# A hybrid attention block: one step's difference in a hand-written filler schedule, and a wider share for PE in the last normalisation

## The chip, the core and the metric

The kernel runs on one core of a Trainium2 chip. A core has five engines with their own instruction streams: PE (TensorE, matrix products into the accumulator banks, PSUM), DVE (VectorE), ACT (ScalarE), POOL (GpSimd) and SP (SyncE, which here only issues DMAs). Each engine takes its instructions in program order and waits on semaphores for the others. The metric is the time of one execution in device microseconds; lower is better.

## The reference

One layer of an encoder block on 1024 tokens of width 1024, float32 in and out. One projection gives the queries, keys, values and gates of two groups of heads:

```python
h = jnp.einsum('bsd,de->bse', x, w_in[layer])
q_a, k_a, v_a, z_a, q_b, k_b, v_b, z_b = jnp.split(h, SPLIT_POINTS, axis=-1)
y_a = neighborhood_attention(q_a, k_a, v_a, rel_bias)      # per head; 8 heads, window 8 x 16 on a 16 x 64 grid, learned bias
y_b = windowed_gqa_with_sink(rotary(q_b), rotary(k_b), v_b, sink)  # 8 query heads, 2 key heads, |i - j| <= 128
mixed = jnp.concatenate([y_a * silu(z_a), y_b * silu(z_b)], axis=-1)
y = jnp.einsum('bse,ed->bsd', mixed, w_out[layer])
x = layer_norm(DEEPNORM_ALPHA * x + y, ln_gain, ln_bias)
```

All heads are 64 wide. The last line, the normalisation over the 1024 columns of a row, is what the second part of the change concerns; the projections of `k_a` and `q_a` are what the first part concerns.

## The kernel before, in words

To keep float32 accuracy with 16-bit products, every operand is held as a high and a low float16 part, and a product is three matmuls: high x high, high x low, low x high.

**Projection.** The 2688 columns besides the values are cut into 21 pieces of 128 columns, named in `ORDER` (L30): `zb0`, `z0`, ... `k3`, `q3`, `z3`. The digit is a pair of heads; `k`, `q`, `z` belong to group "a" (neighbourhood attention), names with `b` to group "b". `project` (L358) makes one piece in two halves of 512 tokens, each 8 k-tiles x 3 products = 24 matmuls of 512 columns into one bank (L379), then `evac` hands the bank to ACT and DVE: for `q` and `k`, ACT writes the high part (L257) and DVE the low part (L263), for each of the two heads; for `k`, POOL then copies each part to the other half of the partitions (L295). For a gate `z`, ACT and DVE compute the SiLU (L341, L342). The weights of a piece are split in two halves by `w_split`: ACT makes the high part (L199), POOL the low one (L204, L205). The last eight pieces' weights were loaded earlier, for their sums, and stay on the chip.

**Attention.** The first six pieces are projected before it. The other 15 (`FILL`) are fillers: `project` is a generator that gives up control after every matmul, and the main loop pumps it a few matmuls at a time between the pieces of attention, to keep PE busy. The loop has 128 steps, one for each unit: a unit is 128 queries of one head, 64 units of group "b" first, then 64 of "a", 16 for each pair of heads. At step i it emits, in this order:

- the scores of unit i on PE, two matmuls (L816, L817), and on DVE bias, minimum and scale into `sn` (L826);
- when it is due, on PE the transposes of an earlier output (L901) and the value products of four units that are 9 to 6 steps old (L881, 36 matmuls);
- for unit i-1, ACT's high part (L852), DVE's low part (L853) of the probabilities, and a DMA transpose of both (L856), issued on SP;
- fillers, then ACT's exponential of unit i (L842), queued work of the splits, and fillers again.

Unit 112 is the first that uses `k3` and `q3` (its step calls `need` for their splits), unit 113 the first that uses the second half of `q3`. `z3` is needed when the first output of the pair is gated. Units of "a" need their bias tables (loaded on SP at L784 seven steps ahead, scaled on POOL at L788) and gathered values `va` (loaded on SP at L740). The order of all this is written out by hand: from here up to the end of attention each engine executes in the order in which the program emits. SP issues transposes, `va`, bias and output-weight loads in one queue.

How many fillers a step gets is set by `FILL_AT` (L36): entry n is the step at which filler n starts, and it is spread evenly until the next entry. Entries 12, 13, 14 and 15 are `k3`, `q3`, `z3` and the first output tiles. `pump_to(u)` pumps the total due by step u.

**Output.** Eight row tiles of 128 tokens. The first banks of the output projection (L1031) are fillers at the end of attention (`out_head`); `final` does the rest. After the residual (L1077, with column sums at L1080), rows are normalised. For tiles 0 to 6 `norm` shares the work among DVE, ACT and POOL. For the last tile nothing is left to hide behind, so `norm_last` splits its 1024 columns in three, at `WP` (L51):

- HP, the first `WP` columns: POOL has multiplied them by the gain (`norm_ahead`, L1099) as soon as their half of the row was there. PE then computes scale, shift and bias as three float32 products into one bank: identity x bias ahead of time (L1104), and with two diagonal matrices `dr` and `dn` (reciprocal deviation, and minus mean times it; made on ACT at L1109, L1110) `dr` x row (L1111) and `dn` x gain (L1112). ACT copies the bank (L1114) and stores it from its own queue (L1118).
- H0, the next 256 columns, and H1, the rest: DVE computes both in two operations each (L1106 and L1113, then L1116), and SP stores them (L1117).

The last tile's second half of output columns comes in three pieces of 256, 128 and 128 columns.

Of the kernel before, what the change touches and what calls it, by code (L numbers as in the profile page):

```python
# [32 lines left out]
NS = 21 - NPRO  # L33
NR = 8
FILL = ORDER[NPRO:]
FILL_AT = [0, 8, 17, 25, 33, 41, 49, 57, 66, 74, 81, 89, 97, 105, 112, 121, 123.5, 126, 128, 131, 136]  # L36
ZTAG = {"z3": "zv", "zb3": "zc", "z2": "zs", "zb1": "zd", "zb2": "ze"}
KO = (2, 3, 4, 5, 6, 7, 0, 1)
X1_AT = ((0,), (1,), (2,), (3, 4), (5,), (6, 7), (), ())
# [8 lines left out]
M_AT = [105, 112, 118, 120]  # L48
WO_AT = [67, 71, 75, 79, 84, 88, 93, 98]
WO_LD = [16, 22, 19, 25, 36, 39, 42, 45, 48, 112, 116, 28, 130, 130, 130, 130]  # L50
WP = 256  # L51
WIN0 = (0, 8, 24, 40)
WINW = (24, 32, 32, 24)
NROW = (11, 12)
# [7 lines left out]
def hybrid_block(ctx, tc, xT, x, wt, wv, wo, bias, sink, gain, lbias, cos, sin, bmask, out):  # L62
# [856 lines left out]
    def pump_to(u):  # L919
        n = 0  # L920
        for k, c in enumerate(FILL_N):
            u0, u1 = FILL_AT[k], FILL_AT[k + 1]
            n += int(c * min(max((u - u0) / (u1 - u0), 0), 1))
# [124 lines left out]
    def final():  # L1048
# [33 lines left out]
        def row_stats(t):  # L1082
            mv = fp.tile([128, 2], F32, tag="mv", name="mv")
            nc.vector.bn_aggr(mv, stats[t][:, :8 if t == 7 else 2, :])  # L1084
            sd = fp.tile([128, 1], F32, tag="sd", name="sd")
            nc.scalar.activation(sd, mv[:, 1:2], AF.Sqrt, bias=eps)  # L1086
            return mv, sd
# [7 lines left out]

        HP, H0, H1 = slice(0, WP), slice(WP, WP + 256), slice(WP + 256, 1024)

# [3 lines left out]
        def norm_last(t):  # L1101
            ts = slice(128 * t, 128 * t + 128)
            xr = xrs[t]
            nc.tensor.matmul(pn[:, :WP], identf, bb[:, HP], start=True, stop=False)  # L1104
            mv, sd = row_stats(t)
# [4 lines left out]
            nc.scalar.activation(dn, identf, AF.Copy, scale=nmr)  # L1110
            nc.tensor.matmul(pn[:, :WP], dr, xr[:, HP], start=False, stop=False)  # L1111
            nc.tensor.matmul(pn[:, :WP], dn, gb[:, HP], start=False, stop=True)  # L1112
            nc.vector.scalar_tensor_tensor(xr[:, H1], xr[:, H1], mv[:, 0:1], gb[:, H1], op0=ALU.subtract, op1=ALU.mult)  # L1113
            nc.scalar.copy(xr[:, HP], pn[:, :WP])  # L1114
            for h in (H0, H1):
# [209 lines left out]
```

## Time and profile before

| | us |
|---|---|
| median of 3 runs | 446.71 |
| lowest and highest | 446.0, 447.76 |
| the profiled execution's own time | 446.49 |
| its span, first to last instruction | 444.7 |

The page of the profile gives busy times, the chain of work that ended last, and the costliest groups of instructions; a group's line is `line engine op out<-in xcount`. The timeline lists instructions with start and duration in microseconds, merged where they follow each other, and in brackets the engine's idle time before and who ended it. The view of waits gives for each pair, waiting engine and line `<-` releaser, the total, the number of times and the longest. Matmuls are pipelined: a 512-column matmul shows some 0.38 us from start to end, while the next one starts much earlier. A row of SP is the issue of a DMA, not the transfer; the time from issue to landing is given apart. In a table by windows the columns are the window, its length, the busy time (and count) of PE, PE's weight loads, DVE, ACT and POOL, the granted clock of PE, the DMA share and GB/s.

### The profile page before, as it was taken

What the parts mean: (1) busy time and instruction counts of PE and PEld (TensorE: products, weight loads), DVE (VectorE), ACT (ScalarE), POOL (GpSimd) and SP (SyncE); (2) the same over time, 40 slices, a digit from 0 to 9 for tenths busy, and PEclk for the clock granted to TensorE, in tenths of its full rate; (3) what the DMA queues carried; (4) which work ended last, traced back from release to release, by engine and by line L of the source; (5) the groups of instructions that cost most, each with busy time, mean ns of one, the idle gap of its engine ahead of it and who ended that gap; (6) DMA issues with size and microseconds to landing.
All of it is one profiled execution on the core that took longest, in us unless ns stands there. A gap on an engine that the chain in (4) does not pass through costs nothing.

```text
span 444.7 us, 9505 instructions
## 1 busy us (share of the span) xinstructions
PE 437.5 (98%) x3289; PEld 255.5 (57%) x3289; DVE 344.2 (77%) x849; ACT 308.3 (69%) x700; POOL 221.6 (50%) x235
## 2 busy tenths in 40 slices
PE   9999999999999999999999999999999999999994
PEld 8997754444445565655565655656555654444453
DVE  5978967438986898887988888888878837589944
ACT  5759789766499988887868887888778946302401
POOL 0110074646839558866506767765574405205740
PEclk9999999999999999999999999999999999999997
DMA  8921469984659999587978899998999998103612
GB/s 272 390 91 60 145 235 339 336 292 169 213 127 214 206 190 181 98 162 143 164 127 175 169 182 180 213 170 213 192 204 253 167 172 347 55 0 102 232 69 72
DMA packets 133841, 81.39 MB, mean 183 GB/s; under 512 B 101280, under 2 KB 113440, under 8 KB 133536
## 3 DMA queue, kind: packets, MB, share of 16 engines
q1 hardware_dynamic: 133648, 80.64, 75.4%
q8 instruction: 26, 0.43, 0.4%
q14 instruction: 23, 0.19, 0.2%
q10 hardware_dynamic: 144, 0.13, 0.1%
HBM read 50.34 MB, written 9.96 MB: 136 GB/s over the span
## 4 chain that ended last, share of the span: by engine, by line
PE 91%; DMA 3%; POOL 3%; DVE 1%; issue 1%; ACT 1%; SPq 0%; POOLq 0%; DVEq 0%; ACTq 0%
PE ps_pj L379 44%; PE ps_s L1031 9%; PE ps_s L486 6%; PE ps_t L881 6%; PE ps_pj L1031 5%; PE ps_t L1031 5%; PE ps_s L816 4%; PE ps_s L817 4%; PE ps_pj L486 3%; PE ps_t L486 3%; DMA bias<-in_bias 3%; PE ps_t L901 1%; POOL wl L205 1%; PE ps_t L412 1%; POOL ks L295 1%
## 5 line engine op out<-in xcount | busy, mean ns | idle before, releaser
L379 PE MATMUL ps_pj<-xf,wh 128*128 128x512 f16 x672 | 202.1, 379 | 0.1
L379 PE MATMUL ps_pj<-xf,wl 128*128 128x512 f16 x336 | 127.3, 379 | 0.0
L379 PEld LDWEIGHTS <-wh 128*128 128x128 f16 x672 | 63.7, 98 | 60.4 <-DVE ks L263 0.5
L842 ACT ACTIVATE ps_s<-sn,nm 128x385 f32<-128x385 f32 (+3 forms) x128 | 70.1, 548 | 25.1 <-DVE nm L826 24.6
L853 DVE SCALAR_TENSOR_TENSOR split<-ps_s,split 128x384 f16<-128x384 f32 (+2 forms) x128 | 65.7, 513 | 27.5 <-ACT split L852 25.9
L1031 PEld LDWEIGHTS <-m 128*128 128x128 f16 x432 | 40.0, 98 | 41.1 <-DVE m L939 0.2
L852 ACT ACTIVATE split<-ps_s 128x384 f16<-128x384 f32 (+2 forms) x128 | 57.8, 452 | 2.5 <-DMA tr<-split 0.2
L204 POOL TENSOR_SCALAR wr<-wr,wsc 128x512 f32<-128x512 f32 x26 | 20.6, 791 | 68.1 <-ACT wh L199 61.6
L379 PEld LDWEIGHTS <-wl 128*128 128x128 f16 x336 | 32.9, 98 | 37.4
L826 DVE CUSTOM_DVE_ANT_0 sn<-ps_s,bm,nsk 128x384 f32<-128x384 f32 (+1 forms) x64 | 40.7, 636 | 2.0 <-PE ps_s L817 1.7
L1031 PE MATMUL ps_s<-wo,m 128*128 128x512 f16 (+1 forms) x192 | 40.8, 366 | 0.0
L816 PE MATMUL ps_s<-ks,qs 128*128 128x384 f16 (+4 forms) x128 | 39.2, 306 | 0.3 <-DVE qs L263 0.3
L817 PE MATMUL ps_s<-ks,qs 128*128 128x384 f16 (+4 forms) x128 | 39.2, 306 | 0.0
L826 DVE CUSTOM_DVE_ANT_0 sn<-ps_s,bias,sg 128x264 f32<-128x264 f32 (+1 forms) x64 | 35.0, 547 | 4.5 <-issue 1.5
L881 PEld LDWEIGHTS <-tr 128*128 128x128 f16 (+1 forms) x1104 | 36.6, 98 | 2.2
L205 POOL TENSOR_TENSOR wl<-wr,wh 128x512 f16<-128x512 f32 x26 | 32.7, 1257 | 2.2
L788 POOL TENSOR_SCALAR bias<-bias,rsg 128x552 f32<-128x552 f32 (+1 forms) x24 | 19.1, 797 | 23.8 <-DMA bias<-in_bias 22.6
L295 POOL COPY ks<-ks 64x512 f16<-64x512 f16 x40 | 26.0, 661 | 7.1 <-DVE ks L263 2.8
L1086 ACT ACTIVATE sd<-mv,eps 128x1 f32<-128x1 f32 x8 | 2.4, 295 | 36.5 <-DVE mv L1084 35.2
L1031 PE MATMUL ps_pj<-wo,m 128*128 128x512 f16 (+1 forms) x144 | 26.2, 326 | 0.0
L1130 POOL TENSOR_TENSOR xr<-xr,gb 128x512 f32<-128x512 f32 x7 | 9.8, 1396 | 32.4 <-ACT xr L1127 32.4
L842 ACT ACTIVATION_READ_ACCUMULATOR ps_s<-sn,nm 128x1 f32 x128 | 24.4, 190 | 0.0
(188 smaller groups left out, 813.8 us busy)
## 6 DMA issues: line engine op xcount, KB each, us to landing
ws<-in_wt SPq DMA_DIRECT2D x15, 512.0 KB, 5.9
wr<-in_wt SPq DMA_DIRECT2D x26, 256.0 KB, 3.6
wor<-in_wo SPq DMA_DIRECT2D x22, 256.0 KB, 3.5
bias<-in_bias SPq DMA_DIRECT2D x16, 276.0 KB, 3.3
xr<-in_x SPq DMA_DIRECT2D x8, 512.0 KB, 9.6
out<-xr SPq DMA_DIRECT2D x15, 256.0 KB, 2.1
bias<-in_bias SPq DMA_DIRECT2D x8, 368.0 KB, 3.8
wvraw<-in_wv SPq DMA_DIRECT2D x9, 320.0 KB, 5.8
```

Of the source, the lines that this page charges most:

```text
L205: nc.gpsimd.tensor_sub(l, raw, h)
L295: nc.gpsimd.tensor_copy(t[o, sl], t[a, sl])
L379: nc.tensor.matmul(ps, a[:, k % 4, :], mv, start=(k == 0 and i == 0), stop=(k == KT - 1 and i == 2))
L486: nc.tensor.matmul(ps[:, :320], lh[:, ts], rh[:, cs], start=(k == ko[0] and i == 0), stop=(k == ko[-1] and i == 2))
L816: nc.tensor.matmul(ps[:, :m], q, sl[0], start=True, stop=False)
L817: nc.tensor.matmul(ps[:, :m], q, sl[1], start=False, stop=True)
L826: nc.vector.tensor_tensor_reduce(sn[:, :m], ps[:, :m], bias_t, sg[:, c:c + 1], init, op0=ALU.add, op1=ALU.min, accum_out=nm)
L842: nc.scalar.activation(pt[:, :m], sn[:, :m], AF.Exp, bias=nm, scale=-1.0, accum_out=sm[:, k:k + 1])
L852: nc.scalar.activation(hl[:, :m, 0, :c], src, AF.Copy, scale=PSCALE)
L853: nc.vector.scalar_tensor_tensor(hl[:, :m, 1, :c], src, PSCALE, hl[:, :m, 0, :c], op0=ALU.mult, op1=ALU.subtract)
L881: nc.tensor.matmul(ps[:, HD * m:HD * m + HD], a, b_, start=(i == 0), stop=(i == len(mms) - 1))
L1031: nc.tensor.matmul(ps, lh[:, ts], rh[:, cs], start=(e == EO[0] and i == 0), stop=(e == EO[-1] and i == 2))
```

## The change

Two entries of `FILL_AT` are one lower: `k3` is spread over the steps 97 to 104 instead of 97 to 105, `q3` over 104 to 111 instead of 105 to 112, and `z3` over 111 to 121 instead of 112 to 121. Nothing before step 97 or after step 121 is emitted at another place. `WP` goes from 256 to 384: HP has 384 columns, H0 stays at 256 (columns 384 to 639), and H1 shrinks from 512 to 384. The number of instructions is the same.

```diff
-FILL_AT = [0, 8, 17, 25, 33, 41, 49, 57, 66, 74, 81, 89, 97, 105, 112, 121, 123.5, 126, 128, 131, 136]
+FILL_AT = [0, 8, 17, 25, 33, 41, 49, 57, 66, 74, 81, 89, 97, 104, 111, 121, 123.5, 126, 128, 131, 136]
...
-WP = 256
+WP = 384
```

## The prediction

> **What bounds the kernel now.** I read the page first: busy time by engine and the chain of waits, for what carries the span.
>
> ```profile
> span 444.7 us, 9505 instructions
> PE 437.5 (98%) x3289; PEld 255.5 (57%) x3289; DVE 344.2 (77%) x849; ACT 308.3 (69%) x700; POOL 221.6 (50%) x235
> PE 91%; DMA 3%; POOL 3%; DVE 1%; issue 1%; ACT 1%; SPq 0%; POOLq 0%; DVEq 0%; ACTq 0%
> ```
>
> PE is the bound, so the change, which adds next to no PE work before the last rows, can only move the time through moments in which PE stands still. The view of waits, PE alone, lists them:
>
> ```profile
> PE ps_t L1111 <- ACT dr L1109: 1.8, 1, 1.8
> PE ps_s L816 <- DVE qs L263: 0.3, 1, 0.3
> ```
>
> There are two of interest, and each part of the change sits on one. The timeline around the second, PE's own, shows the scores of units 110, 112 and 113 (their first matmul, L816), and two fillers of the projection before unit 113:
>
> ```profile
> 327.05 0.28 PE L816 MATMUL ps_s<-ks,qs 128*128 128x264 f16 x1
> ...
> 330.54 0.28 PE L816 MATMUL ps_s<-ks,qs 128*128 128x264 f16 x1
> ...
> 331.41 0.59 PE L379 MATMUL ps_pj<-xf,wh 128*128 128x512 f16 x2
> 332.26 0.30 PE L816 MATMUL ps_s<-ks,qs 128*128 128x288 f16 x1 [0.26 <-DVE qs L263]
> ```
>
> One filler's price is in the chain of waits, six in a row:
>
> ```profile
> 287.39 1.29 PE ps_pj L379 x6
> ```
>
> That is 0.216 us each. Unit 113 could have started at 331.41 + 2 x 0.216 = 331.84; it started at 332.26. PE lost 0.42 us there. The timelines of ACT and DVE say why:
>
> ```profile
> 330.91 0.58 ACT L257 ACTIVATE qs<-ps_pj 64x512 f16<-64x512 f32 x1
> ```
>
> ```profile
> 327.57 0.49 DVE L826 CUSTOM_DVE_ANT_0 sn<-ps_s,bias,sg 128x264 f32<-128x264 f32 x1 [0.82 <-POOL wl L205]
> ...
> 327.99 0.55 DVE L853 SCALAR_TENSOR_TENSOR split<-ps_s,split 128x384 f16<-128x384 f32 x1
> ...
> 331.52 0.68 DVE L263 SCALAR_TENSOR_TENSOR qs<-ps_pj,qs 64x512 f16<-64x512 f32 x1 [0.81 <-ACT qs L257]
> ```
>
> The second half of q3 is complete only when unit 112 starts; its high part comes out on ACT until 331.49, its low part on DVE until 332.20, and unit 113 is the first reader of that half.
>
> **Part 1: k3 in 7 steps, q3 a step sooner, z3 over 10 steps.** No instruction is added. What moves on PE: after step 105, k3 and q3 stand (110-104) x 48/7 = 41 matmuls into q3 by step 110, where it was (110-105) x 48/7 = 34. So the scores of units 106 to 111 come behind 7 more fillers: 7 x 0.216 = 1.5 us later. By step 121 z3 is complete in both, and the shift is 0.
>
> What it saves: q3 ends before unit 111's scores. From there to unit 113 lie two pairs of scores and 9 of z3's fillers, about 2.4 us; in the trace the last low part was 332.20 - 330.54 = 1.7 us behind q3's end. The low part then has some 0.7 us to spare, and the wait goes: -0.42 us.
>
> Evacuations and weights: k3's and q3's splits on ACT and DVE (eight each), z3's weight splits (two on ACT, four on POOL) and the eight copies of k3 on POOL move ahead with the fillers; none issues a DMA here, since the last sixteen weight halves are on the chip already, and SP's order is unchanged. On POOL the bias of unit 112 drops behind z3's second weight half. POOL's list in the trace, all of these included, was through with the bias of unit 114 at
>
> ```profile
> 328.52 0.88 POOL L788 TENSOR_SCALAR bias<-bias,rsg 128x736 f32<-128x736 f32 x1
> ```
>
> that is by 329.40; the first reader, unit 112, now comes later than 330.54. I cost this at nothing; if the cover went, PE would wait the overrun at unit 112.
>
> What it costs: SP's queue. Transposes of the probabilities, the `va` loads and bias loads are issued there in order. Its timeline, the transpose of unit 109 first, then the rows behind it, and the last ten:
>
> ```profile
> 328.60 1.33 SPq L856 DMA_TRANSPOSE tr<-split  x1
> ```
>
> ```profile
> 329.99 0.57 SPq L740 DMA_DIRECT2D va<-vwin  x1
> 330.65 0.52 SPq L784 DMA_DIRECT2D bias<-in_bias  x1
> ...
> 347.56 14.93 SPq L856 DMA_TRANSPOSE tr<-split  x10
> ```
>
> From 328.60 to 362.49 the rows follow each other within 0.1 us, save 0.3 us once: the queue is full to the last transpose, and a delay ahead of it stays. And at 328.60 it has no backlog: unit 109's low part ended at 327.99 + 0.55 = 328.54, and that DVE instruction stands behind unit 110's `sn` (327.57), which stands behind unit 110's scores (327.05). Those scores now come 1.5 us later, so this transpose does too. Before it the queue was behind its data, so 0.1 of the 1.5 may be made up; I take a delay d = 1.4 us for all transposes from unit 109 on. Bounds: 0 (the data were early in some way the row hides) and 1.5; 1.4 is nearest the rows.
>
> Who waits: the value product of four units (L881, 36 matmuls over 1.05 us, nine a unit), on PE. Its two tight places, from PE's timeline, and the transposes of their fourth units (115 and 123) with the time to landing, each alone in a window:
>
> ```profile
> 346.96 1.22 PE L881 MATMUL ps_t<-va,tr 96*128 96x64 f16 x36
> ...
> 358.56 1.22 PE L881 MATMUL ps_t<-va,tr 96*128 96x64 f16 x36
> ```
>
> ```profile
> L856 SPq DMA_TRANSPOSE tr<-split x1: 1211/1211/1211, 341.5 to 341.5; - x1
> ...
> DMA to landing us min/median/max: 4.8/4.8/4.8
> ```
>
> ```profile
> L856 SPq DMA_TRANSPOSE tr<-split x1: 2615/2615/2615, 354.5 to 354.5; - x1
> ...
> DMA to landing us min/median/max: 4.2/4.2/4.2
> ```
>
> The fourth unit's matmuls start 27/36 x 1.05 = 0.79 us in: at 347.75 against a landing at 341.5 + 4.8 = 346.3, slack 1.45; and at 359.35 against 354.5 + 4.2 = 358.7, slack 0.6. With d = 1.4 the second lands at 360.1, 0.8 us behind the old start, and PE waits there whether or not it had gained 0.42 earlier. So part 1 nets max(-0.42, d - 0.6) = +0.8 us: the stall of unit 113 goes, and is late again, larger, under the transposes. Behind it PE has out-projection matmuls whose inputs come later by d too; in the trace PE waits for none of them, and I cost that at nothing.
>
> **Part 2: 384 columns instead of 256 on PE in the last rows.** The end of the timeline:
>
> ```profile
> 433.07 0.73 POOL L1099 TENSOR_TENSOR xr<-xr,gb 128x256 f32<-128x256 f32 x1 [0.21 <-DVE stats L1080]
> ```
>
> ```profile
> 436.76 0.65 PE L1104 MATMUL ps_t<-bb,identf 128*128 128x256 f32 x2
> ...
> 438.09 0.48 DVE L1106 SCALAR_TENSOR_TENSOR xr<-xr,mv,gb 128x256 f32<-128x256 f32 x1
> ...
> 438.76 0.74 DVE L1113 SCALAR_TENSOR_TENSOR xr<-xr,mv,gb 128x512 f32<-128x512 f32 x1
> ...
> 439.23 0.67 PE L1111 MATMUL ps_t<-xr,dr 128*128 128x256 f32 x2 [1.81 <-ACT dr L1109]
> ...
> 439.73 0.96 PE L1112 MATMUL ps_t<-gb,dn 128*128 128x256 f32 x2
> ...
> 440.78 0.37 ACT L1114 COPY xr<-ps_t 128x256 f32<-128x256 f32 x1 [1.41 <-PE ps_t L1112]
> 441.18 0.37 ACTq L1118 DMA_DIRECT2D out<-xr  x1
> ```
>
> ```profile
> 440.59 1.52 SPq L1117 DMA_DIRECT2D out<-xr  x1
> ```
>
> Time to landing, of that last SP store and of ACT's store:
>
> ```profile
> DMA to landing us min/median/max: 3.2/3.2/3.2
> ```
>
> ```profile
> DMA to landing us min/median/max: 2.0/2.0/2.0
> ```
>
> DVE's branch ends at 440.59 + 3.2 = 443.8, PE's at 441.18 + 2.0 = 443.2: slack 0.6. DVE's two ops of 512 columns become 384: half way between 0.48 and 0.74, each saves 0.13, so its store goes 0.26 sooner (443.5). POOL's product grows to about 1.1 us, done five microseconds ahead; L1104 grows by a third of a microsecond before `dr` exists. But L1111 and L1112 stand behind `dr`: from 439.23 to 440.69 they take 1.46 us for 256 columns. With 384 they add half of that at most, 0.73, and 0.5 if the fixed ends are left out; I take 0.55. The copy adds 0 to 0.18, taken 0.1. ACT's store is issued 0.65 later and lands at 443.9 with 2.0, the wider store perhaps 0.1 more. The last landing moves from 443.8 to about 443.95: +0.15 us. Bounds -0.26 (PE's branch stays short) and +0.6 (0.73 + 0.18, and a landing 0.3 slower).
>
> Two rows of the clock by windows bear on it:
>
> ```profile
> 439.00:440.00 1.00, 0.77 (x3) 0.72 (x4) 1.00 (x3) 0.37 (x2) 0.00 (x0) 0.92 0.00 0
> 440.00:441.00 1.00, 0.69 (x2) 0.00 (x0) 0.56 (x1) 0.22 (x1) 0.00 (x0) 0.50 0.26 79
> ```
>
> The granted clock halves at 439.84, some 2.4 us after L1104 ended (437.41), so L1112 already runs at half clock, and the added columns mostly too; 1.46 us contains that. [...]
>
> **Sum.** The profiled execution took 446.49 us, span 444.7. 446.49 + 0.8 + 0.15 = 447.4. It lies 0.2 under the median 446.71, so on that scale 447.6; I say 447.5.
>
> **Rivals.** (1) The transposes are not late enough to matter, d under 0.2: the stall is simply gone, -0.42, and the tail -0.26 to +0.15: 446.0 to 446.5. For it: softmax of earlier units was behind DVE and ACT, not PE, so their order may absorb some of 1.5 us. Against it: the zero backlog at 328.60. d = 0.6 decides between gain and loss.
> (2) The change doesn't do what it says: unit 113 waits as before, since DVE takes the low part behind unit 111's `sn` and split, which now come later. Only 0.7 us are to spare. Up to 0.4 more at unit 113, but d - 0.6 still rules: 447.5 to 448.
> (3) Slower beyond 0.5%: PE's clock drops in the middle. The place is the value product at 358.56; the tail shows a drop after 2.4 us without matmuls. It decides when transposes come 3.0 us late there, which needs a second row like the 2.6 us transpose at 354.5. The price: 2.4 us of standing still, and then each filler at 0.43 in place of 0.216; for ten fillers 2.2 us: 451. [...]
>
> **How the numbers follow.** Forecast 0.55, rival 1 0.3, rival 2 0.1, rival 3 0.05. Differences under 0.5% (2.2 us) are about what a measurement of this kernel can tell from no change, and the runs shown spread from 446.0 to 447.76. All but rival 3 lie within it: same 0.92, slower 0.06, faster 0.02. The range runs from rival 1's end, 446.0, to rival 2 with the tail's upper bound, 448.5, with 0.2 us on either side, the distance of the profiled execution from the median.
>
> **What would show it.** Right: no wait of L816 for L263 at unit 113; transposes of units 109 to 127 issued 1.4 us later against PE's fillers; a new wait of PE before the fourth quarter of the next to last L881 group; L1114 0.55 us later behind `dr`, and ACT's store landing last. Wrong: unit 109's transpose issued by 329.0, or SP's queue with gaps behind it, which would give the time back; or L1117's store still landing last.

## The result and the profile after

The changed kernel took 447.42 us (median of 20 runs, 446.25 to 448.46); the kernel before, run beside it, 446.23 us (20 runs, 445.2 to 447.76). The ratio is 1.0022 with a 95% interval of 1.0012 to 1.0031: about 1.0 us slower (1.2 between the medians), which is less than the 0.5% taken as the bound of "no change". The forecast was 447.5. The profiled execution took 447.68 us with a span of 445.9, against 446.49 and 444.7.

The page of the changed kernel, span and busy times:

```profile
span 445.9 us, 9504 instructions
PE 437.7 (98%) x3289; PEld 254.9 (57%) x3289; DVE 344.0 (77%) x849; ACT 308.1 (69%) x700; POOL 222.0 (50%) x235
```

PE is still the bound, with 0.2 us more work. The view of waits, PE alone (total, times, longest):

```profile
PE ps_t L1111 <- ACT dr L1109: 1.6, 1, 1.6
...
PE ps_t L881 <- DMA tr<-split: 0.6, 1, 0.6
```

The wait of unit 113 for the low part of `q3` (L816 <- L263) is gone, and the value product (L881) waits for a transpose. PE's timeline shows unit 113, and then two of the value products:

```profile
332.45 0.29 PE L816 MATMUL ps_s<-ks,qs 128*128 128x288 f16 x1
...
346.29 0.95 PE L881 MATMUL ps_t<-va,tr 96*128 96x64 f16 x27
347.84 0.44 PE L881 MATMUL ps_t<-va,tr 128*128 128x64 f16 x9 [0.60 <-DMA tr<-split]
...
358.68 1.45 PE L881 MATMUL ps_t<-va,tr 96*128 96x64 f16 x36
```

The first product breaks in two: 27 matmuls, then nine of the fourth unit, 115. At 1.05/36 = 0.029 us each the nine could have started at 346.29 + 0.79 = 347.08; they start at 347.84, so PE lost 0.76 us (the bracket's 0.60 counts from the modelled end of the matmul before, 0.95 us behind 346.29). The other group, with unit 123 as its fourth, takes 1.45 where an undisturbed one takes 1.22: another 0.23. Below, "standing still" is always worked out in this way.

SP's timeline shows why, the transpose of unit 109 first, then those of units 114 and 115 with an output-weight load between them:

```profile
329.86 1.22 SPq L856 DMA_TRANSPOSE tr<-split  x1
...
340.85 1.21 SPq L856 DMA_TRANSPOSE tr<-split  x1
342.12 1.54 SPq L951 DMA_DIRECT2D wor<-in_wo  x1
343.76 1.21 SPq L856 DMA_TRANSPOSE tr<-split  x1
```

Up to unit 97 the two kernels are the same. The first matmul of its scores, in the kernel before and in the changed one, shows the execution after 0.25 us ahead there:

```profile
300.58 0.29 PE L816 MATMUL ps_s<-ks,qs 128*128 128x288 f16 x1
```

```profile
300.33 0.29 PE L816 MATMUL ps_s<-ks,qs 128*128 128x288 f16 x1
```

With that taken out, unit 109's transpose is 329.86 + 0.25 - 328.60 = 1.51 us later than before, and unit 115's 343.76 + 0.25 - 341.49 = 2.5 later. The same stretch of SP in the kernel before:

```profile
341.49 1.21 SPq L856 DMA_TRANSPOSE tr<-split  x1
342.79 1.41 SPq L740 DMA_DIRECT2D va<-vwin  x1
```

Here the slow issue (1.41 in place of about 0.55) stands behind unit 115's transpose. In the changed kernel the slow one (1.54) stands ahead of it.

The end of the timeline of the changed kernel:

```profile
439.04 0.40 ACT L1109 ACTIVATE dr<-identf,rstd 128x128 f32<-128x128 f32 x1 [0.24 <-DVE rstd L1091]
...
439.59 0.89 PE L1111 MATMUL ps_t<-xr,dr 128*128 128x384 f32 x2 [1.59 <-ACT dr L1109]
...
440.31 0.81 PE L1112 MATMUL ps_t<-gb,dn 128*128 128x384 f32 x2
441.21 0.48 ACT L1114 COPY xr<-ps_t 128x384 f32<-128x384 f32 x1 [1.47 <-PE ps_t L1112]
441.72 0.37 ACTq L1118 DMA_DIRECT2D out<-xr  x1
```

The DMA view of the last microseconds, 439.4 to 445 (KB, us from issue to landing; the row of q8 is an instruction fetch, with packets, MB and share of the DMA engines):

```profile
q8 instruction: 1, 0.02, 1.1%
...
out<-xr SPq DMA_DIRECT2D x1, 192.0 KB, 1.9
out<-xr ACTq DMA_DIRECT2D x1, 192.0 KB, 3.2
out<-xr SPq DMA_DIRECT2D x1, 128.0 KB, 1.8
```

ACT's store lands last, at 441.72 + 3.2 = 444.9, and it is the slow one of the three. The same view of the kernel before (439 to 444) has the slow ones elsewhere:

```profile
q8 instruction: 1, 0.02, 1.8%
...
out<-xr SPq DMA_DIRECT2D x1, 256.0 KB, 3.2
out<-xr SPq DMA_DIRECT2D x1, 128.0 KB, 2.9
out<-xr ACTq DMA_DIRECT2D x1, 128.0 KB, 2.0
```

From the end of `dr` to the end of the span it is 445.9 - 439.44 = 6.5 us after and 444.7 - 439.08 = 5.6 before. The span's difference of 1.2 us is thus: -0.25 ahead of unit 97, -0.42 at unit 113, +0.76 + 0.23 at the transposes, +0.82 in the tail, which makes 1.14.

### The profile page after: what moved, and what is told of

Read it like the earlier page. It is cut to its first block, busy times and chain, and to the rows that moved or that the text cites. A ratio compares the mean times of both kernels' runs of the same rounds, so it can differ in the third digit from the quotient of the medians.

```text
span 445.9 us, 9504 instructions
## 1 busy us (share of the span) xinstructions
PE 437.7 (98%) x3289; PEld 254.9 (57%) x3289; DVE 344.0 (77%) x849; ACT 308.1 (69%) x700; POOL 222.0 (50%) x235
## 4 chain that ended last, share of the span: by engine, by line
PE 96%; DMA 2%; DVE 1%; ACT 0%; issue 0%; DVEq 0%; SPq 0%; ACTq 0%
PE ps_pj L379 48%; PE ps_s L1031 8%; PE ps_t L881 7%; PE ps_s L486 6%; PE ps_pj L1031 5%; PE ps_t L1031 5%; PE ps_s L816 4%; PE ps_s L817 4%; PE ps_pj L486 3%; PE ps_t L486 3%; DMA tr<-split 2%; PE ps_t L901 1%; PE ps_t L412 1%; PE ps_t L1111 0%; DVE ks L263 0%
## 5 line engine op out<-in xcount | busy, mean ns | idle before, releaser
L816 PE MATMUL ps_s<-ks,qs 128*128 128x384 f16 (+4 forms) x128 | 39.2, 307 | 0.0
L881 PEld LDWEIGHTS <-tr 128*128 128x128 f16 (+1 forms) x1104 | 36.8, 98 | 3.1 <-DMA tr<-split 0.9
```

The costliest lines, as they stand in the source:

```text
L816: nc.tensor.matmul(ps[:, :m], q, sl[0], start=True, stop=False)
L881: nc.tensor.matmul(ps[:, HD * m:HD * m + HD], a, b_, start=(i == 0), stop=(i == len(mms) - 1))
```

## The experiments

The theory: each part costs something for a reason of its own. The earlier `q3` delays the transposes in SP's full queue; the wider `WP` lengthens the branch that ends last. Rivals: one part alone makes the whole difference; the transposes' delay is beside the point and the fillers cost it in another way. The fillers alone, the columns alone, the fillers with two loads moved and the doubled dose ran on one chip beside the kernel before (446.35 us there), the other four on a second chip (446.7 us there).

**One part alone: the fillers.**

```diff
-FILL_AT = [..., 97, 105, 112, 121, ...]
+FILL_AT = [..., 97, 104, 111, 121, ...]
 WP = 256
```

> The schedule's part alone (FILL_AT of the changed kernel, WP = 256). My theory: the scores of units 106 to 111 come 1.5 us later, the transposes of units 109 to 127 follow, and PE waits for them at the fourth quarters of two value products (0.76 + 0.23 us in the changed kernel's trace) while the wait of 0.42 us at unit 113 goes: net +0.6 us against the kernel before (ratio 1.0013), with the same two waits in its trace. Rival: the loss of the changed kernel is all in the last rows; then this one is 0.4 us faster than before.

Measured: 447.47 us, ratio 1.0026 (1.0011 to 1.0041). PE's timeline at unit 115, and SP's:

```profile
346.73 0.69 PE L881 MATMUL ps_t<-va,tr 96*128 96x64 f16 x18
347.64 0.44 PE L881 MATMUL ps_t<-va,tr 128*128 128x64 f16 x9 [0.22 <-DMA tr<-split]
348.98 0.44 PE L881 MATMUL ps_t<-va,tr 128*128 128x64 f16 x9 [0.90 <-DMA tr<-split]
```

```profile
341.05 3.43 SPq L856 DMA_TRANSPOSE tr<-split  x1
344.54 0.57 SPq L951 DMA_DIRECT2D wor<-in_wo  x1
345.21 1.21 SPq L856 DMA_TRANSPOSE tr<-split  x1
```

The third and the fourth unit's quarters both wait: PE stands still 0.39 + 1.07, and 0.26 in the next group, 1.72 in all. Less the 0.42 saved that is +1.3 us in the trace, and +1.1 between the medians (0.5 to 1.8 by the ratio's interval), more than the +0.6 expected. The places differ too: PE waits for the transposes of units 114, 115 and 119, and not for unit 123's. The slow issue was unit 114's transpose here, with 3.43 us. The rival that the whole loss lies in the last rows falls.

**One part alone: the columns.**

```diff
-WP = 256
+WP = 384
```

> The last rows' part alone (WP = 384, FILL_AT of before). By the prediction +0.15 us. By the changed kernel's trace, where ACT's store took 3.2 us to land instead of 2.0, +0.8 us (1.0018) if that belongs to the 384 columns or to ACT's queue; if it was that execution's chance, between 0 and +0.3. The wait of 0.42 us at unit 113 stays in either case.

Measured: 446.79 us, ratio 1.0011 (1.0001 to 1.0020). The stall at unit 113 is there (0.42). PE also stands still for 1.47 - 1.22 = 0.25 us at one value product, ahead of the places that this document is about:

```profile
316.92 1.47 PE L881 MATMUL ps_t<-va,tr 96*128 96x64 f16 x36
```

It waits there for unit 99's transpose, which took 2.75 us to issue (at 311.97) and landed at 317.91; the matmuls that read it start at 317.96. So a slow issue can cost PE a little on the old schedule as well; this 0.25 is not the columns' price. By the medians the fillers carry the larger part of the difference and the columns about 0.4 us. By the times alone the fillers could be all of it, since this run's interval only just leaves out 1; that the columns cost something of their own rests on the tails below. The DMA view of the columns alone, 439.9 to 444.1, where no instruction fetch lies among the stores:

```profile
out<-xr SPq DMA_DIRECT2D x1, 192.0 KB, 1.9
out<-xr ACTq DMA_DIRECT2D x1, 192.0 KB, 1.9
out<-xr SPq DMA_DIRECT2D x1, 128.0 KB, 1.8
```

**The suspected cause taken away.** SP's queue holds two output-weight loads among these transposes, which nothing reads before the output. They are issued behind the last transpose instead, with the fillers of the first experiment and 256 columns; this is the third kernel below. Nothing changes on PE, ACT or DVE in what is emitted.

```diff
-WO_LD = [16, 22, 19, 25, 36, 39, 42, 45, 48, 112, 116, 28, ...]
+WO_LD = [16, 22, 19, 25, 36, 39, 42, 45, 48, 130, 130, 28, ...]
```

> The schedule's part with two output-weight loads taken out from between the transposes on SP's queue (WO_LD[9] and [10] at step 130 instead of 112 and 116; they are then issued behind the last transpose). If the loss is the transposes' delay on SP's queue, two issue slots of 0.6 us or more are given back, 0.6 us ahead of unit 111's transpose and as much ahead of unit 115's: the wait at unit 115's transpose goes, that at unit 123's shrinks below 0.3, and with the 0.42 us of unit 113 the kernel is between 0.4 us faster and equal to the one before (0.6 to 1.0 us below the schedule's part alone). Rival, the loss is not SP's queue (ACT, DVE or the transfer itself are late): no more than 0.2 us between the two.

Measured: 445.84 us, ratio 0.9997 (0.9982 to 1.0013); 1.6 us less than the fillers alone on the same chip by the medians and 1.3 by the ratios, where 0.6 to 1.0 was expected, since the fillers alone had lost more than expected. Its waits of PE have no L881 and no L816:

```profile
PE ps_t L1111 <- ACT dr L1109: 1.8, 1, 1.8
...
PE ps_pj L379 <- DVE ks L263: 0.3, 1, 0.3
```

SP's timeline, the transpose of unit 115:

```profile
342.10 2.33 SPq L856 DMA_TRANSPOSE tr<-split  x1
```

This execution is 0.51 us behind before unit 97, so unit 115's transpose comes 342.10 - 0.51 - 341.49 = 0.1 later than in the kernel before, although unit 109's is late here as in the others (330.62). Two issues taken out ahead of it have given the delay back, and the loss went with it: the way from the fillers to the lost time is SP's queue. The rival that the fillers cost it in another way falls.

**The control: the two loads alone**, with the fillers of the kernel before.

> The two output-weight loads taken out from between the transposes, on the schedule of before (FILL_AT and WP of before). Theory: before the change PE waits for no transpose, so a shorter queue on SP alone is worth nothing: within 0.2 us of before, the wait of 0.42 us at unit 113 still there and no wait of L881. Rival, the loads themselves cost PE time (or their late arrival does): 0.4 us or more in either direction.

Measured: 446.25 us, ratio 0.9996 (0.9985 to 1.0007). PE's timeline at unit 113 still shows

```profile
331.64 0.59 PE L379 MATMUL ps_pj<-xf,wh 128*128 128x512 f16 x2
332.49 0.30 PE L816 MATMUL ps_s<-ks,qs 128*128 128x288 f16 x1 [0.25 <-DVE qs L263]
```

that is 332.49 - (331.64 + 2 x 0.216) = 0.42, and no wait of L881 is there. The ratio puts it 0.2 us below the kernel before, with both signs in its interval; the medians lie 0.45 apart, more than the 0.2 expected. PE's timeline decides: its scores run 0.24 us behind the kernel before at unit 97 and the same 0.24 at unit 127, so the moved loads alone gave PE nothing. Without the earlier fillers there is nothing at the transposes to be won.

**The dose doubled.** `k3` and `q3` two steps sooner, loads where they were.

```diff
-FILL_AT = [..., 97, 105, 112, 121, ...]
+FILL_AT = [..., 97, 103, 110, 121, ...]
```

> A second dose: k3 over steps 97 to 103, q3 over 103 to 110, z3 over 110 to 121, WP = 256. Unit 110's scores come 14 fillers, 3.0 us, later than before instead of 1.5. Theory: transposes from unit 109 on are 2.9 to 3.3 us late; behind the slack of 0.6 at unit 123 that makes +2.3 to +2.7 us against before (1.005 to 1.006). Rival, the delay is made up on SP's queue or by shorter waits elsewhere: within 0.3 us of the first dose.

Measured: 448.40 us, ratio 1.0048 (1.0033 to 1.0063), +2.05 us, a little under the 2.3 to 2.7 expected. Rows of its SP and PE timelines:

```profile
331.72 1.21 SPq L856 DMA_TRANSPOSE tr<-split  x1
```

```profile
348.79 0.44 PE L881 MATMUL ps_t<-va,tr 128*128 128x64 f16 x9 [0.93 <-DMA tr<-split]
...
354.99 0.43 PE L881 MATMUL ps_t<-va,tr 96*128 96x64 f16 x9 [0.42 <-DMA tr<-split]
```

Unit 109's transpose is 3.0 us late (331.72 - 0.09 - 328.60), twice 1.5. PE stands still 2.37 us over five places, so net +1.95 in the trace. Time grows with the dose, and three fourth quarters carry most of it (1.82 of the 2.37; two third quarters carry the rest). The second step added 0.9 us between the medians, not the whole 1.5, so the rival that it stays within 0.3 us of the first dose falls.

**The third kernel again**, the same code on the second chip, since its interval held both signs.

> The earlier schedule with the two loads moved, once more, to narrow its interval. Theory: neither the wait at unit 113 nor one for a transpose: 0.4 us faster than before (ratio 0.999), and 0.4 us faster than the moved loads on the old schedule.

Measured: 445.84 us, ratio 0.9978 (0.9963 to 0.9993); no standing still at unit 113 or at a transpose. That is 0.4 us less than the moved loads on the old schedule, as expected, and 0.9 less than the kernel before by the medians, where 0.4 was expected. Its tail and DMA view (438 to 442) serve as the undisturbed tail with 256 columns:

```profile
438.24 0.67 PE L1111 MATMUL ps_t<-xr,dr 128*128 128x256 f32 x2 [1.81 <-ACT dr L1109]
...
438.75 0.59 PE L1112 MATMUL ps_t<-gb,dn 128*128 128x256 f32 x2
...
439.83 0.37 ACTq L1118 DMA_DIRECT2D out<-xr  x1
```

```profile
out<-xr SPq DMA_DIRECT2D x1, 256.0 KB, 2.1
out<-xr SPq DMA_DIRECT2D x1, 128.0 KB, 1.7
out<-xr ACTq DMA_DIRECT2D x1, 128.0 KB, 2.1
```

**The size of the columns, to the other side and further.** `WP = 192` on top of the third kernel, and `WP = 512` on the kernel before.

> The same with WP = 192. In three executions with 256 columns ACT's store was issued 1.74 us after the end of dr and landed last; SP's second store landed 0.2 us ahead. If PE's branch is the longer one already at 256 columns, 64 columns less take 0.25 us from it and put 0.13 on DVE's: 0.1 us from the end of dr to the end of the span, SP's store last. If DVE's branch is the longer one, as the prediction read it, 0.13 us more. In time, no difference that rounds can show.

> A second dose of the last rows' part: WP = 512 on the schedule of before; H1 has 256 columns. From the end of dr to the end of the span it was 4.8 to 4.9 us with 256 columns (three executions, 5.6 in a fourth) and 5.1 with 384 (6.4 in a second). If PE's branch is the bound, each 128 columns put 0.43 us on L1111 and L1112 and 0.11 on the copy: 5.6 us, and 0.8 to 1.0 us over before (1.002). If the tail is set by what a store takes to land, whatever the columns: no more than 0.3 over before.

Measured: 446.03 us, ratio 0.9989 (0.9976 to 1.0002), with 192, and 447.32 us, 1.0013 (1.0000 to 1.0025), with 512. PE's last row and ACT's store with 512 columns:

```profile
440.69 1.02 PE L1112 MATMUL ps_t<-gb,dn 128*128 128x512 f32 x2
...
442.42 0.37 ACTq L1118 DMA_DIRECT2D out<-xr  x1
```

From the timelines and the times to landing, in us behind the end of `dr` on ACT:

| columns, kernel | last matmul ends | ACT's store issued, landed | SP's second store landed | end of span |
|---|---|---|---|---|
| 256, before | 1.61 | 2.10, 4.15 | 4.74 | 5.63 |
| 256, the third kernel again | 1.25 | 1.74, 3.84 | 3.61 | 4.79 |
| 384, after | 1.67 | 2.27, 5.50 | 3.09 | 6.45 |
| 384, columns alone | 1.67 | 2.27, 4.14 | 3.10 | 5.09 |
| 512 | 2.10 | 2.81, 4.82 | 2.79 | 5.89 |
| 192 | 1.03 | 1.47, 3.77 | 4.45 | 5.40 |

The other four executions with 256 columns agree with the second row to 0.01 us in the landings. Three executions of the ten, those of before, after and 192, have a 16 KB instruction fetch among the stores, and they are the three with a store that took over 2.5 us to land. In the other seven ACT's store lands last: 3.84 with 256, 4.14 with 384, 4.82 with 512. So the tail grows with the columns, and the rival that a store's landing alone sets it falls. With 512 the tail is 5.89, over the 5.6 expected, and yet the median is only 0.6 us over the kernel before, under the 0.8 to 1.0 expected; why is not shown. With 192 the slow store hides which branch would have ended last, so that stays open; the intervals of its ratio and of the same kernel with 256 columns overlap.

## Why the prediction was right, point by point

**Unit 113's wait.** Right: the wait is gone in every kernel with the earlier fillers, and 0.42 us stands there in every one without. The rival that it stays, behind a later `sn`, fell.

**The delay of the transposes.** Right in mechanism and size at its start: 1.51 us at unit 109 in all five kernels with these fillers, where 1.4 was taken, since nothing was made up. DVE's low part of unit 109 ended at 329.80 and the transpose was issued at 329.86, so the queue had no backlog there. The rival with transposes not late enough fell too.

**Where PE waits.** This step failed in its place. Two tight places were named, and only the second, unit 123 with a slack of 0.6, was to bind; unit 115 had 1.45, which 1.4 would not use up. The premise "a delay ahead of it stays" took the delay as constant along the queue. It was 2.5 us at the issue of unit 115's transpose, outside the bounds of 0 to 1.5, because the order of slow and quick issues changed. The transfer landed in 4.0 us instead of 4.8, so the landing was 1.76 later, and 1.76 - 1.45 = 0.3 over the old start: with the 0.42 that PE had gained, the 0.76 seen. At unit 123 the transpose was issued at 356.88 and landed 2.8 us later, at 359.65; that is 359.65 + 0.25 - 358.7 = 1.2 late.

**The size of part 1.** The term +0.8 was d - 0.6 with d = 1.4. With the 1.2 found at unit 123 it gives 0.6, and PE's net in this execution is 0.76 + 0.23 - 0.42 = 0.57: in this execution the formula holds and its input was 0.2 too large. In the execution of the fillers alone, where units 114, 115 and 119 bound PE instead, the net was 1.3, and 1.1 between its medians, since the slow issue lay ahead of unit 115 with 3.4 us. So +0.8 is a fair middle, and the scatter that the sum did not have is where the slow issues fall.

**The tail.** The sum was near and its premise wrong. "DVE's branch ends at 443.8, PE's at 443.2: slack 0.6" was read from one execution in which both of SP's stores landed slowly. In all seven executions whose stores are undisturbed ACT's store lands last, by 0.23 us with 256 columns (3.84 against 3.61). So added columns cost from the first one on: 4.14 - 3.84 = +0.3 us for 384, where +0.15 was taken. The columns alone measured about +0.4. The added time of PE was 1.67 - 1.25 = 0.42 where 0.55 was taken, since the row had the half clock in it (0.50 from 439.84 on); the wider copy took 0.1, as taken; the store itself was 0.2 quicker to land. The sign that L1114 starts 0.55 us later behind `dr` did not come: it starts 441.21 - 439.44 = 1.77 behind it, against 440.78 - 439.08 = 1.70, since L1112 had run at half clock before. The +0.82 between the two profiled executions is not the price of the columns: in the executions without a fetch these tails are 5.09 and 4.79 long.

**The clock.** It was at 1.00 in the changed kernel until the end, as its windows show (the last value but two is the granted clock):

```profile
440.00:441.00 1.00, 1.00 (x4) 0.37 (x2) 0.66 (x2) 0.00 (x0) 0.00 (x0) 1.00 0.00 0
```

In the kernel before it fell to 0.50 at 439.84, 0.75 us behind `dr` (mean of the span 0.995), in the other nine executions 1.7 us or more behind it, after PE's last matmul, or not at all within the span (means 0.997 to 1.00). The 0.36 us that the drop cost L1112 thus belonged to that one execution. "A drop after 2.4 us without matmuls" was a misreading: L1111 had run from 439.23 on, so PE had stood still for 1.81 us, and gaps of 1.4 to 1.9 us at the same place brought no drop before the last matmul in the other nine; what brought it there stays open. The rival of a clock drop in the middle did not come: the changed kernel's mean granted clock was 1.00 and no wait there exceeded 1.1 us. What a stop of 2.4 us would have brought there, no run shows.

**The sum.** The columns' +0.3 (tails) to +0.4 (medians) and the fillers' +0.6 (the changed kernel's trace) to +1.1 (medians) make +0.9 to +1.5; measured +1.2 between the medians. That the forecast lay within 0.1 us owes something to chance, since part 1 was sized well for another place and the tail by a premise that fell.

## What to carry to other kernels

A stall taken away by doing work sooner pushes other work later: look for the queue without a backlog at that moment, follow the delay to each reader, and subtract that reader's slack. In the full queue of this case neither the delay (1.2 to 2.5 us in one execution) nor the slack (0.6 and 1.45) was the same for all of them. The cure may lie in that queue too, and be cheap. Here two loads that nobody waits for, moved behind the last transpose, turned a ratio of 1.0026 into 0.9997 and 0.9978 (445.84 us both times), the quickest of the kernels tried, though by less than the 0.5% told apart here. Which of two branches ends last at the end of a kernel should be read from several executions before a slack between them is spent.

## What the runs showed of the hardware

Instruction fetches of 16 KB lie on a DMA queue of their own (q8), five of them between 298 and 356 us, 10 to 17 us apart and at the same places to 1.4 to 3.3 us in every execution, and the slow issues lie beside them. The DMA view of the changed kernel from 342 to 343.7 has one, with the 1.54 us load:

```profile
q8 instruction: 1, 0.02, 4.6%
...
wor<-in_wo SPq DMA_DIRECT2D x1, 256.0 KB, 5.0
```

That of the fillers alone, from 341 to 344.5, has one with unit 114's transpose:

```profile
q8 instruction: 1, 0.02, 4.5%
...
tr<-split SPq DMA_TRANSPOSE x1, 6.5
```

Over the ten executions SP issues 500 DMAs in this stretch. Of the 44 that took at least 0.15 us longer than the median of their kind 40 overlap such a fetch, and of the other 456 only 34 do. In the tail all five stores that took over 2.5 us to land do, in three executions. Not beside each fetch lies a slow issue: that at 327.7 in the kernel before has none. The two coincide in ten traces, but no experiment moved a fetch, so the cause stays open. For a reading it means that a transpose's 2.6 us or a store's 3.2 us in one execution need not be the kernel's own price, and belongs in the range, not in the sum.
